# Hybrid S5 / gMLP trunk: second-token transposes inside a product, last columns in two parts, S5 tiles pipelined, x on the ScalarE queue, first products by quarters

## The chip, the cores and the metric

One Trainium2 chip, one of its cores. The metric is device time in microseconds (us) of one execution. The kernel before took 971.5 us in the median of three runs (970.46 to 971.52).

## What is computed

The input x is 256 tokens by 1024 columns, float32. Two layers follow, each of three sub-layers of the form "residual plus branch, then layer normalisation" (cut from the reference):

```python
for i in range(DEPTH):                                    # DEPTH = 2
    h = _layernorm(DN_ALPHA * h + 0.5 * _swiglu(h, ffn_w_in[i, 0], ffn_w_out[i, 0]), ln_g[i, 0], ln_b[i, 0])
    mix = _s5_mixer(h, ...) if i % 2 == 0 else _gmlp_mixer(h, ...)
    h = _layernorm(DN_ALPHA * h + mix, ln_g[i, 1], ln_b[i, 1])
    h = _layernorm(DN_ALPHA * h + 0.5 * _swiglu(h, ffn_w_in[i, 1], ffn_w_out[i, 1]), ln_g[i, 2], ln_b[i, 2])

def _swiglu(x, w_in, w_out):                              # 1024 -> 2 x 2816 -> 1024
    gate, up = jnp.split(x @ w_in, 2, axis=-1)
    return (jax.nn.silu(gate) * up) @ w_out
```

The S5 mixer projects in, runs a diagonal complex state-space scan over the tokens, gates the result (`z = y * sigmoid(y @ w_glu + b_glu)`) and projects out. The gMLP mixer projects to u and v, normalises v, mixes its tokens with one 128x128 matrix per head, multiplies by u and projects out. So the order of sub-layers is FFN, S5, FFN, FFN, gMLP, FFN, and the six are called FFN0, S5, FFN1, FFN2, gMLP, FFN3 here.

## The kernel before, in words

**Numbers.** Every float32 product is made of three matmuls on operands split into a high part (rounded to the matmul's type) and a low part (the rest): high x high, high x low, low x high (`mm3`, L201 to L203, with 512 moving columns; `mm3t`, L208 to L210, with 256). The split of a weight block takes a cast on ScalarE (`hi`) and a subtraction on VectorE (`lo`).

**Tokens.** The 256 tokens are two tiles of 128 rows, t = 0 and t = 1, kept in `h[0]` and `h[1]`. A product needs the transposed tokens: `make_xt(t)` lets TensorE transpose eight 128x128 pieces into two PSUM tiles `tps` (L187), ScalarE casts each to the high part (L192), VectorE makes the low part (L193).

**Weights.** `Stream` keeps one list of weight blocks of 128x2048 for the whole program. SyncE's queue loads them (L63) into three `raw` buffers, `split` makes `hi` and `lo` (L88/L89 where the low part is put off to the next tick, `ws.lazy`; L96/L97 otherwise; L106/L107 in quarters at the start; L115/L119 slowly in S5). At most five split blocks are held. `ws.tick(n)` splits n more blocks if that bound allows and runs one piece of background work, which in FFN0 is the preparation of the S5 tables (VectorE L639 to L649, ScalarE L881 and others) and later that of the gMLP. Each engine works through its own queue strictly in the order in which the program was written (`manual_schedule`), so the place of a tick in the code decides what stands behind what.

**An FFN** goes through 11 chunks of 256 hidden units. Chunks 0 and 1 are computed token tile by token tile: in FFN0 by `start_in` (chunk 0) and `chunk_in(1)`, in the other FFNs by `step_in(0, 0)`, `step_in(1, 0)`, then `make_xt(1)`, then `step_in(0, 1)`, `step_in(1, 1)`, each of 8 input pieces k and hence 24 matmuls `ips`. In the second token tile `finish_g` transposes the gated values (L348) after the fourth k. From chunk 2 on weights are stationary (`chunk_in`, L208 to L210), and `step_out(c - 2)` adds a finished chunk to the accumulators `acc`. The last three chunks of the output product are done in `close`: first token tile 0, both halves of 512 columns, then token tile 1. The layer normalisation of a tile (VectorE L239, L240, L247, then L228, L231; GpSimd makes 1/sqrt in two steps, L221 and L222) starts when its halves are done. While TensorE is in token tile 1's last blocks, `make_xt(0)` already turns the normalised token tile 0 for the next sub-layer.

**The start of FFN0** (`start_in`): x and the first weight block come in pieces on SyncE's queue; `ws.early()` issues four small transposes `aps` for the S5 tables (L679, L680), whose results ScalarE copies out (L685 to L691).

**gMLP** begins with `step_v(0, 0)`, `step_v(1, 0)`, `make_xt(1)`, `act_v` of both, then `step_v` of token tile 1; its products are called `zps`.

**The end of S5**: after the gate products (`gacc`, L1148 to L1150) ScalarE makes eight tanh tiles (L1158), and `finish(n)` for n = 0 to 7 multiplies (L1164), casts to the high part (VectorE L1168 for n < 3, ScalarE L1170 from then on) and subtracts (L1171); `rest(1)` after n = 1 and 3 makes a half of a weight block's low part (L119). `close_mixer` then multiplies with `w_out`, in the order of k = n.

Of the kernel before, what the change touches and what calls it, by code (L numbers as in the profile page):

```python
# [16 lines left out]
P = 128  # L17
# [137 lines left out]
def hybrid(ctx: ExitStack, tc: tile.TileContext, a: dict, out: bass.AP, subs=SUBS):  # L155
# [63 lines left out]
    def rstd_of(mv, eps):  # L219
        rstd = st_p.tile([P, 2], F32, tag="rstd", name="rstd")  # L220
        nc.gpsimd.tensor_scalar(rstd[:, 0:1], mv[:, 1:2], eps, 1.0, op0=ALU.add, op1=ALU.mult)  # L221
        nc.gpsimd.tensor_tensor(rstd[:, 1:2], rstd[:, 0:1], mhalf, op=ALU.pow)  # L222
        return rstd[:, 1:2]
# [51 lines left out]

    def close(li, si, acc, blocks, mm, gb, hscale, eps, last):

        order = [(n, j) for n in range(2) for j in range(len(blocks))]
        for t in range(2):
            for n, j in order:  # L280
                for kt in range(2):
                    mm(j, t, n, kt, acc[t][n])
                    if (t, n, j, kt) == (1, 1, len(blocks) - 2, 0) and not last:
# [7 lines left out]
            if t == 1 and not last:  # L291
                ws.tick(1)
            layernorm(t, acc[t], gb, hscale, eps, sums)
            if t == 1 and not last and next_kind[li, si] != "s5":
                ws.tick(1, 4)
            if last:
                for n in range(2):
                    s = slice(512 * n, 512 * n + 512)
                    (nc.sync, nc.scalar)[n].dma_start(out=out[0, P * t:P * t + P, s], in_=h[t][:, s])

    def plan_ffn(li, fi, fine):
# [3 lines left out]
        def add_in(c):  # L305

            ids["in"][c] = []
            for kh in range(2):
# [11 lines left out]
                if step == 1 and kh == 0:  # L320
                    parts[2:2] = [(lambda raw: h[1], a["x"][0, P:2 * P, :])]
# [11 lines left out]
    def ffn(ids, li, si, first, last):  # L333
# [27 lines left out]
        def step_in(c, t):  # L361
            ps = mm_p.tile([P, 512], F32, tag="mm", name="ips")
            in_mm(ids["in"][c], t, ps, range(4))
            if t:
                finish_g()
            ws.tick()
            in_mm(ids["in"][c], t, ps, range(4, KD))
# [3 lines left out]
            ws.tick()  # L371

        def chunk_in(c):

            for m in range(2):
                ps = mm_p.tile([P, 2, SEQ], F32, tag="mm", name="ips")
                for g in range(2):
# [13 lines left out]
                    ws.tick()  # L391
# [17 lines left out]
        def start_in():  # L409
# [5 lines left out]
            split(0)  # L415
            make_xt(0, parts=[1])
            mm(0, 0)
            split(1)
            make_xt(1)
            ws.early()  # L420
            mm(0, 1)
            for k in range(2):
                mm(1, k)
            for k in range(2, 4):
                split(k)
                for t in range(2):
                    mm(t, k)
# [13 lines left out]
        def mm_out(c, t, n, kt, ps):  # L441
            gh, gl = (gts[c, kt][:, j, P * t:P * t + P] for j in range(2))
            wh, wl = ws.get(ids["out"][c])
            s = slice(D * kt + 512 * n, D * kt + 512 * n + 512)
            mm3(ps, gh, gl, wh[:, s], wl[:, s], c == 0 and kt == 0, c == NCH - 1 and kt == 1)
# [12 lines left out]
        if first:  # L458
            start_in()
            ws.lazy = True  # L460
            chunk_in(1)
        else:
            step_in(0, 0)
            step_in(1, 0)
            make_xt(1)
# [888 lines left out]
```

## Time and profile before

| | |
|---|---|
| median of three runs | 971.5 us |
| the profiled execution's own time | 971.83 us |
| its span in the profile | 969.7 us |
| TensorE busy in the span | 944.7 us (97%) |
| VectorE, ScalarE, GpSimd busy | 650.9, 426.5, 162.8 us |
| chain that ended last: TensorE, VectorE, ScalarE | 68%, 8%, 2% of the span |
| weight and other reads from HBM | 184.07 MB |

A row of the timeline gives start and duration in us, engine, line of the kernel, operation, output <- input, shape and count; behind it in brackets the idle time of that engine just before the row and what ended it. Matmuls overlap, so the distance from one start to the next says what a matmul costs, not its duration. PE is TensorE, DVE is VectorE, ACT is ScalarE, POOL is GpSimd, SP is SyncE.

### The profile page before, as it was taken

Reading aid. Unit: us, or ns where it says so; the run is one execution under the profiler, and the core shown is the slowest. Engines: PE = TensorE matmul, PEld = TensorE weight load, DVE = VectorE, ACT = ScalarE, POOL = GpSimd, SP = SyncE. Lnnn points to the kernel's source line nnn. Section 1 sums busy time; section 2 is a strip of 40 time slices with the busy share of each in tenths; the row PEclk is TensorE's granted clock in tenths of the full one; section 3 lists DMA queues with packets and bytes.
Section 4 is the critical chain, followed back from the end, with each engine's and each line's share of the span. In section 5 each row is a group of like instructions: output and inputs, shape, how many; then the busy total and the mean of one; then the engine's idle time right before and its main releaser. Section 6 shows DMA issues by size and latency. Waiting matters only on the chain.

```text
span 969.7 us, 16611 instructions
## 1 busy us (share of the span) xinstructions
PE 944.7 (97%) x6988; PEld 857.9 (88%) x6988; DVE 650.9 (67%) x805; ACT 426.5 (44%) x504; POOL 162.8 (17%) x240
## 2 busy tenths in 40 slices
PE   7999999999999999999999999999999999999996
PEld 5999999978896799999987999999889879999995
DVE  5889998787998774554667636455788866453635
ACT  5465347535342553434433534353445444444430
POOL 1888910011750100000001000000011010000001
PEclk9999999999999999999999999999999999999999
DMA  8887796958646566365547765636357468465521
GB/s 276 219 249 228 237 318 203 315 200 300 208 141 220 174 198 236 132 224 167 185 163 239 255 222 166 225 133 227 121 173 261 130 203 268 138 220 172 184 78 43
DMA packets 133898, 195.10 MB, mean 201 GB/s; under 512 B 7632, under 2 KB 104576, under 8 KB 133824
## 3 DMA queue, kind: packets, MB, share of 16 engines
q1 hardware_dynamic: 129152, 182.61, 56.8%
q0 software_dynamic: 4384, 10.92, 3.9%
q8 instruction: 54, 0.88, 0.4%
q10 hardware_dynamic: 288, 0.52, 0.1%
q14 instruction: 20, 0.16, 0.0%
HBM read 184.07 MB, written 9.96 MB: 200 GB/s over the span
## 4 chain that ended last, share of the span: by engine, by line
PE 68%; DVE 8%; ACT 2%; issue 1%; POOL 1%; DMA 1%; POOLq 0%; DVEq 0%; ACTq 0%
PE ips L210 11%; PE ips L209 11%; PE ips L208 11%; PE acc L201 7%; PE acc L202 7%; PE acc L203 7%; DVE lo L97 3%; PE pps L1080 2%; PE ips L203 1%; ACT hi L96 1%; DVE lo L89 1%; DMA raw<-in_s_w_in 1%; PE ips L201 1%; PE ips L202 1%; PE zps L209 1%
## 5 line engine op out<-in xcount | busy, mean ns | idle before, releaser
L210 PE MATMUL ips<-xt,lo 128*128 128x256 f32 x1184 | 335.2, 283 | 2.2 <-DVE lo L89 2.2
L208 PE MATMUL ips<-xt,hi 128*128 128x256 f32 x1184 | 335.4, 283 | 0.0
L209 PE MATMUL ips<-xt,hi 128*128 128x256 f32 x1184 | 335.0, 283 | 0.0
L89 DVE TENSOR_TENSOR lo<-raw,hi 128x2048 fp32r<-128x2048 f32 x107 | 242.9, 2291 | 8.7 <-ACT hi L88 8.3
L210 PEld LDWEIGHTS ips<-xt,lo 128*128 128x128 f32 x1184 | 227.1, 192 | 2.6 <-DVE lo L89 2.6
L208 PEld LDWEIGHTS ips<-xt,hi 128*128 128x128 f32 x1184 | 227.1, 192 | 1.5
L209 PEld LDWEIGHTS ips<-xt,hi 128*128 128x128 f32 x1184 | 227.1, 192 | 1.4
L88 ACT CAST hi<-raw 128x2048 fp32r<-128x2048 f32 x107 | 203.9, 1909 | 46.4 <-PE acc L203 26.6
L398 DVE TENSOR_TENSOR sgg<-ips,sgg 128x256 f32<-128x256 f32 x74 | 31.1, 420 | 166.1 <-ACT sgg L397 166.0
L201 PE MATMUL acc<-hi,gt 128*128 128x512 f32 x352 | 137.9, 392 | 0.2 <-ACT gt L406 0.2
L202 PE MATMUL acc<-lo,gt 128*128 128x512 f32 x352 | 137.4, 390 | 0.0
L203 PE MATMUL acc<-hi,gt 128*128 128x512 f32 x352 | 137.0, 389 | 0.0
L397 ACT ACTIVATE sgg<-ips 128x256 f32<-128x256 f32 x74 | 28.4, 383 | 216.4 <-PE ips L210 213.5
L221 POOL TENSOR_SCALAR rstd<-mv 128x1 f32<-128x1 f32 x14 | 10.4, 741 | 634.6 <-DVE mv L247 610.8
L97 DVE TENSOR_TENSOR lo<-raw,hi 128x2048 fp32r<-128x2048 f32 (+2 forms) x52 | 89.6, 1754 | 22.7 <-ACT hi L96 22.6
L203 PEld LDWEIGHTS acc<-hi,gt 128*128 128x128 f32 x352 | 66.1, 188 | 14.3 <-DVE gt L407 0.2
L201 PEld LDWEIGHTS acc<-hi,gt 128*128 128x128 f32 x352 | 66.2, 188 | 13.2 <-ACT gt L406 0.6
L202 PEld LDWEIGHTS acc<-lo,gt 128*128 128x128 f32 x352 | 66.3, 188 | 12.2
L96 ACT CAST hi<-raw 128x2048 fp32r<-128x2048 f32 (+2 forms) x52 | 74.5, 1482 | 4.2 <-DMA raw<-in_ffn_w_in 2.5
L407 DVE TENSOR_TENSOR gt<-sgg,gt 128x256 fp32r<-128x256 f32 x74 | 32.4, 438 | 61.8 <-ACT gt L406 61.8
L406 ACT CAST gt<-sgg 128x256 fp32r<-128x256 f32 x74 | 30.1, 406 | 58.2 <-DVE sgg L398 58.2
L201 PE MATMUL ips<-hi,xt 128*128 128x512 f32 x112 | 46.0, 410 | 3.6 <-ACT xt L192 2.3
(229 smaller groups left out, 1222.1 us busy)
## 6 DMA issues: line engine op xcount, KB each, us to landing
raw<-in_ffn_w_in SPq DMA_DIRECT2D x172, 512.0 KB, 5.7
raw<-in_ffn_w_out SPq DMA_DIRECT2D x44, 1024.0 KB, 5.1
raw<-in_g_w_in SPq DMA_DIRECT2D x8, 1024.0 KB, 6.0
rows<-w SPq DMA_DIRECT2D x8, 512.0 KB, 6.3
raw<-in_s_w_in SPq DMA_DIRECT2D x4, 1024.0 KB, 8.4
raw<-in_s_w_glu SPq DMA_DIRECT2D x4, 1024.0 KB, 5.0
w<-rows SPq DMA_DIRECT2D x8, 512.0 KB, 5.8
tc<-tc SPq DMA_DIRECT2D x16, 256.0 KB, 5.5
```

The source lines that it names most:

```text
L88: nc.scalar.copy(hi, raw)
L89: self.unfinished.append(lambda: nc.vector.tensor_tensor(lo, raw, hi.bitcast(F32), op=ALU.subtract))
L96: nc.scalar.copy(hi[:, s], raw[:, s])
L97: eng[p % len(eng)].tensor_tensor(lo[:, s], raw[:, s], hi[:, s].bitcast(F32), op=ALU.subtract)
L201: nc.tensor.matmul(ps, xh, wh, start=start, stop=False)
L202: nc.tensor.matmul(ps, xh, wl, start=False, stop=False)
L203: nc.tensor.matmul(ps, xl, wh, start=False, stop=stop)
L208: nc.tensor.matmul(ps, wh, xh, start=start, stop=False)
L209: nc.tensor.matmul(ps, wh, xl, start=False, stop=False)
L210: nc.tensor.matmul(ps, wl, xh, start=False, stop=stop)
L398: nc.vector.tensor_tensor(g, ps[:, 1], sg, op=ALU.mult)
L407: nc.vector.tensor_tensor(x[:, 1], g, x[:, 0].bitcast(F32), op=ALU.subtract)
```

## The change

Five groups of edits.

1. *Start.* x is loaded by three DMAs on ScalarE's queue, no longer on SyncE's among the weight pieces. `start_in` multiplies each quarter of the first weight block with token tile 0 as soon as it is split, turns token tile 1 only after that, and issues `ws.early()` after token tile 1's four products. `ws.lazy` is set one step later, inside `chunk_in(1)`, and that step splits two blocks at once.
2. *Second tokens.* In `step_in(1, 0)` and `step_v(1, 0)` the call `make_xt(1)` stands after the fifth of the eight k. Before it no new block is split (`split=0` in `step_in(0, 0)` and `step_v(0, 0)`).
3. *1/sqrt.* The first of the two steps (add eps) is done by VectorE instead of GpSimd, in all 14 normalisations.
4. *End of S5.* The subtraction of tile n is issued after the multiplication of tile n + 1; for n = 3 and 5 GpSimd does it; the products z lie in four buffers instead of two; the halves of the weight split come after n = 4 and 5.
5. *Last sub-layer.* `close_last` makes columns 512 to 1023 of token tile 1 in two products of 256 columns, which go to PSUM tiles of their own (`ops`) for the last three chunks; what the accumulator held before is added to the residual ahead of them. Statistics, normalisation and output of that tile are in parts too.

```diff
 def rstd_of(mv, eps):
-    nc.gpsimd.tensor_scalar(rstd[:, 0:1], mv[:, 1:2], eps, 1.0, op0=ALU.add, op1=ALU.mult)
+    nc.vector.tensor_scalar(rstd[:, 0:1], mv[:, 1:2], eps, 1.0, op0=ALU.add, op1=ALU.mult)
     nc.gpsimd.tensor_tensor(rstd[:, 1:2], rstd[:, 0:1], mhalf, op=ALU.pow)
...
+def close_last(acc, blocks, mm, gb, hscale, eps):
+    for t in range(2):
+        parts = [(0, 512), (512, 512)] if t == 0 else [(0, 512), (512, 256), (768, 256)]
+        step = parts[-1][1]
+        if t == 1:
+            s = slice(512, D)
+            nc.vector.scalar_tensor_tensor(r[:, s], in0=h[t][:, s], scalar=hscale, in1=acc[t][1], op0=ALU.mult, op1=ALU.add)
+        for i, (c, w) in enumerate(parts):
+            ps = acc[t][n] if w == 512 else mm_p.tile([P, 512], F32, tag="mm", name="ops")[:, 0:w]
+            for j in range(len(blocks)):
+                for kt in range(2):
+                    mm(j, t, n, kt, ps, (c % 512, w), w < 512 and j == 0 and kt == 0)
...
-def step_in(c, t):
+def step_in(c, t, mid=None, split=1):
     ps = mm_p.tile([P, 512], F32, tag="mm", name="ips")
-    in_mm(ids["in"][c], t, ps, range(4))
+    cut = 5 if mid else 4
+    in_mm(ids["in"][c], t, ps, range(cut))
+    if mid:
+        mid()
     if t:
         finish_g()
-    ws.tick()
-    in_mm(ids["in"][c], t, ps, range(4, KD))
+    ws.tick(split)
+    in_mm(ids["in"][c], t, ps, range(cut, KD))
     in_act(c, t, ps)
     if t == 1:
         done(ids["in"][c])
-    ws.tick()
+    ws.tick(split)
...
-                    ws.tick()
+                    if first and (c, m, g) == (1, 0, 0):
+                        ws.tick(2)
+                        ws.lazy = True
+                    else:
+                        ws.tick()
...
             split(0)
+            mm(0, 0)
             make_xt(0, parts=[1])
-            mm(0, 0)
-            split(1)
+            for k in range(1, 4):
+                split(k)
+                mm(0, k)
             make_xt(1)
+            for k in range(4):
+                mm(1, k)
             ws.early()
-            mm(0, 1)
-            for k in range(2):
-                mm(1, k)
-            for k in range(2, 4):
-                split(k)
-                for t in range(2):
-                    mm(t, k)
...
-            step_in(0, 0)
-            step_in(1, 0)
-            make_xt(1)
+            step_in(0, 0, split=0)
+            step_in(1, 0, lambda: make_xt(1))
...
-        pend = [step_v(0, 0), step_v(1, 0)]
-        make_xt(1)
+        pend = [step_v(0, 0, split=0), step_v(1, 0, lambda: make_xt(1))]
...
-            z = buf["o"][n % 2][:, 0].rearrange("p q k -> p (q k)")
+            z = buf["o"][n % 2][:, n // 2 % 2].rearrange("p q k -> p (q k)")
...
-            V.tensor_tensor(yx(n, 1), z, yx(n, 0).bitcast(F32), op=SUB)
+            return lambda: (G if n in (3, 5) else V).tensor_tensor(yx(n, 1), z, yx(n, 0).bitcast(F32), op=SUB)
...
+        second = lambda: None
         for n in range(CT):
-            finish(n)
-            if n in (1, 3):
+            x = finish(n)
+            second()
+            second = x
+            if n in (4, 5):
                 rest(1)
+        second()
...
-            nc.sync.dma_start(out=h[0][:, s], in_=a["x"][0, 0:P, s])
-        if kinds[0] != "ffn":
-            nc.sync.dma_start(out=h[1], in_=a["x"][0, P:2 * P, :])
+            nc.scalar.dma_start(out=h[0][:, s], in_=a["x"][0, 0:P, s])
+        nc.scalar.dma_start(out=h[1], in_=a["x"][0, P:2 * P, :])
```

How the instructions stand afterwards is shown at three places. The first is ScalarE's queue at the very start: `xt` are the tokens' casts, `hi_154` the four quarters of weight block 0, `hi_222` those of block 1, and the rows on `aps` the copies for the S5 tables. Before:

```order
L192 CAST xt<-tps 128x512
L106 CAST hi_154<-raw_101 128x512
L192 CAST xt<-tps 128x512
L106 CAST hi_154<-raw_101 128x512
L192 CAST xt<-tps 128x512 x2
L676 COPY s5a<-dt_131 32x128
L685 COPY ch<-aps 128x64
L687 COPY ldt<-aps 128x32
L690 COPY dg<-aps 128x8
L691 ACTIVATE dg<-aps 128x8
L106 CAST hi_154<-raw_101 128x512 x2
```

and with the change, where the token tile 1 casts, and with them the copies, come after all four quarters:

```order
L192 CAST xt<-tps 128x512
L106 CAST hi_154<-raw_102 128x512
L192 CAST xt<-tps 128x512
L106 CAST hi_154<-raw_102 128x512 x3
L192 CAST xt<-tps 128x512 x2
L713 COPY s5a<-dt_131 32x128
L722 COPY ch<-aps 128x64
L724 COPY ldt<-aps 128x32
L727 COPY dg<-aps 128x8
L728 ACTIVATE dg<-aps 128x8
L106 CAST hi_222<-raw_107 128x512 x4
```

The copies and the quarters of block 1 behind them now wait for the casts of token tile 1 and for `aps`, where before only two quarters of block 0 stood between.

The second place is TensorE at the same start. `h_95` is token tile 1, and `aps` the transposes whose results ScalarE copies. Before, from the third matmul of the first product on:

```order
L203 MATMUL ips<-hi_154,xt 128x512
L187 MATMUL tps<-ident,h_95 128x128 x8
L679 MATMUL aps<-ident,s5a 128x32 x3
L680 MATMUL aps<-ident,s5a 128x16
L201 MATMUL ips<-hi_154,xt 128x512
L202 MATMUL ips<-lo_155,xt 128x512
L203 MATMUL ips<-hi_154,xt 128x512
```

and with the change, from the last product of token tile 1 with block 0 on:

```order
L201 MATMUL ips<-hi_154,xt 128x512
L202 MATMUL ips<-lo_155,xt 128x512
L203 MATMUL ips<-hi_154,xt 128x512
L716 MATMUL aps<-ident,s5a 128x32 x3
L717 MATMUL aps<-ident,s5a 128x16
L201 MATMUL ips<-hi_222,xt 128x512
L202 MATMUL ips<-lo_223,xt 128x512
L203 MATMUL ips<-hi_222,xt 128x512
```

What moved is `aps`: nine matmuls of token tile 0 and twelve of token tile 1 with block 0 are now ahead of it, and the first matmul with block 1 stands right behind it.

The third place is VectorE at the entry of FFN1. The four 128x512 rows are the quarters of the second block of chunk 1, the 128x2048 row is the next whole block. Before:

```order
L231 SCALAR_TENSOR_TENSOR h_95<-r,rstd,bet 128x512 x2
L97 TENSOR_TENSOR lo_3723<-raw_3589,hi_3722 128x512 x4
L97 TENSOR_TENSOR lo_3751<-raw_3602,hi_3750 128x2048
L358 TENSOR_TENSOR sgg<-ips,sgg 128x256 x2
L193 TENSOR_TENSOR xt<-tps,xt 128x512 x2
L352 TENSOR_TENSOR gt<-tps,gt 128x128 x4
```

and with the change, where that whole block stands behind the two `xt` rows, and the second gated product `sgg` behind the block:

```order
L231 SCALAR_TENSOR_TENSOR h_95<-r,rstd,bet 128x512 x2
L97 TENSOR_TENSOR lo_3723<-raw_3589,hi_3722 128x512 x4
L390 TENSOR_TENSOR sgg<-ips,sgg 128x256
L193 TENSOR_TENSOR xt<-tps,xt 128x512 x2
L97 TENSOR_TENSOR lo_3796<-raw_3602,hi_3795 128x2048
L390 TENSOR_TENSOR sgg<-ips,sgg 128x256
L384 TENSOR_TENSOR gt<-tps,gt 128x128 x4
```

The whole block went from ahead of both gated products and the token rows to between the token rows and the second gated product.

More of the change, by code (lines that the diff above doesn't have):

```diff
@@ L276, in close @@
     def close(li, si, acc, blocks, mm, gb, hscale, eps, last):
+        if last:
+            return close_last(acc, blocks, mm, gb, hscale, eps)
         order = [(n, j) for n in range(2) for j in range(len(blocks))]
@@ L282, in close @@
                     mm(j, t, n, kt, acc[t][n])
-                    if (t, n, j, kt) == (1, 1, len(blocks) - 2, 0) and not last:
+                    if (t, n, j, kt) == (1, 1, len(blocks) - 2, 0):
                         make_xt(0, next_kind[li, si] == "s5")
@@ L290, in close @@
                     sums = layernorm_half(t, acc[t][0], 0, hscale)
-            if t == 1 and not last:
+            if t == 1:
                 ws.tick(1)
             layernorm(t, acc[t], gb, hscale, eps, sums)
-            if t == 1 and not last and next_kind[li, si] != "s5":
+            if t == 1 and next_kind[li, si] != "s5":
                 ws.tick(1, 4)
[L296 to L299, printed above, removed]
     def plan_ffn(li, fi, fine):
@@ L439, in start_in, with mm_out @@
             done(ids["in"][0])
-        def mm_out(c, t, n, kt, ps):
+        def mm_out(c, t, n, kt, ps, cols=(0, 512), start=False):
             gh, gl = (gts[c, kt][:, j, P * t:P * t + P] for j in range(2))
             wh, wl = ws.get(ids["out"][c])
-            s = slice(D * kt + 512 * n, D * kt + 512 * n + 512)
-            mm3(ps, gh, gl, wh[:, s], wl[:, s], c == 0 and kt == 0, c == NCH - 1 and kt == 1)
+            s = slice(D * kt + 512 * n + cols[0], D * kt + 512 * n + sum(cols))
+            end = NCH - 4 if last and (t, n) == (1, 1) and cols[1] == 512 else NCH - 1
+            mm3(ps, gh, gl, wh[:, s], wl[:, s], start or c == 0 and kt == 0, c == end and kt == 1)
         def step_out(c, t):
@@ L479, in ffn @@
         c0 = NCH - 3
-        close(li, si, acc, [ids["out"][c] for c in range(c0, NCH)], lambda j, t, n, kt, ps: mm_out(c0 + j, t, n, kt, ps),
+        close(li, si, acc, [ids["out"][c] for c in range(c0, NCH)], lambda j, *args: mm_out(c0 + j, *args),
               gb, 2 * ALPHA, 4 * EPS, last)
```

37 lines of the change are left out of this document (29 added, 8 removed).

## Prediction

> **What bounds the kernel now.** I read the page's busy times first, then a table of windows, then the timeline where a window loses TensorE time. The page says:
>
> ```profile
> span 969.7 us, 16611 instructions
> PE 944.7 (97%) x6988; PEld 857.9 (88%) x6988; DVE 650.9 (67%) x805; ACT 426.5 (44%) x504; POOL 162.8 (17%) x240
> ```
>
> TensorE is busy 944.7 of 969.7 us. The change removes no product, so only TensorE's 25 us of idle time, and matmuls that run slowly, are to be had. The windows (span, then busy PE, PEld, DVE, ACT, POOL) show where:
>
> ```profile
> 0.00:16.00 16.00, 10.35 (x32) 7.55 (x33) 6.81 (x11) 8.49 (x18) 3.61 (x13) 1.00 0.88 267
> 290.00:305.00 15.00, 13.39 (x60) 9.57 (x59) 10.88 (x22) 6.40 (x14) 0.00 (x0) 1.00 0.73 232
> 305.00:340.00 35.00, 33.27 (x154) 26.61 (x153) 27.13 (x37) 14.83 (x20) 4.46 (x6) 1.00 0.56 180
> 940.00:970.00 30.00, 21.29 (x114) 18.12 (x112) 12.92 (x22) 1.20 (x3) 3.38 (x4) 0.93 0.09 35
> ```
>
> The start idles 5.7 us, the end of S5 1.6, the entry of FFN1 1.7 and the end 8.7; the entries of S5, FFN2 and gMLP are single waits, quoted below. The change touches each. The sum is made against the profiled execution, 971.83 us (span 969.7 and 2.1 around it). The median is 0.33 lower; I lower the result by the same.
>
> **Second tokens.** At the entry of FFN2, TensorE turns token tile 1, then waits for its casts:
>
> ```profile
> 515.83 4.69 DVE L97 TENSOR_TENSOR lo<-raw,hi 128x512 fp32r<-128x512 f32 x5
> 520.44 0.75 DVE L358 TENSOR_TENSOR sgg<-ips,sgg 128x256 f32<-128x256 f32 x2
> 518.99 0.40 PE L203 MATMUL ips<-hi,xt 128*128 128x512 f32 x1
> 519.22 1.03 PE L187 MATMUL tps<-ident,h 128*128 128x128 f32 x8
> 519.86 1.07 ACT L192 CAST xt<-tps 128x512 fp32r<-128x512 f32 x2
> 521.01 0.47 PE L201 MATMUL ips<-hi,xt 128*128 128x512 f32 x1 [0.75 <-ACT xt L192]
> 521.84 0.50 PE L203 MATMUL ips<-hi,xt 128*128 128x512 f32 x1
> 711.96 0.50 PE L201 MATMUL zps<-hi,xt 128*128 128x512 f32 x1 [0.96 <-DVE xt L193]
> ```
>
> Matmuls of 512 columns stand 0.23 apart (518.99, 519.22). From 519.22 to 521.84 are 2.62 us for eight transposes (0.9) and two matmuls (0.46): 1.3 lost. Turned after the fifth k, the transposes start nine matmuls (2.05 us) earlier, at 517.1, and the casts are done at 517.1 + 0.64 + 1.07 = 518.8, while nine matmuls run to 520.1. VectorE has the four quarters (4.69 less one whole block of 2.29) by 518.2, one gated product by 518.5, both token rows by 519.9. So the second tile's product starts at 520.1 and waits for nothing: 1.4 us gained with the small gaps.
>
> But a new wait comes. The whole block (2.29) now stands between the token rows and the second gated product. ScalarE casts it at 518.8 to 520.7, VectorE splits it to 523.0, the product follows to 523.4. `finish_g` wants it after twelve matmuls, at 522.8: 0.5 lost. So 0.95 at each FFN entry behind another sub-layer, and three of them: **2.85**, between 0 (the block's load late) and 4.2 (no new wait). At gMLP nothing of the second product is wanted there: the 0.96 of idle goes, and an estimated 0.2 by which the first matmuls behind such a wait run slower (0.50 against 0.40), **1.15**, between 0.9 and 1.3.
>
> **1/sqrt.** GpSimd's first step goes to VectorE:
>
> ```profile
> 501.44 0.21 DVE L247 BATCH_NORM_AGGREGATE mv<-bst 128x2 f32<-128x12 f32 x1
> 501.69 1.42 DVE L228 SCALAR_TENSOR_TENSOR r<-r,mv,gam 128x512 f32<-128x512 f32 x2
> 503.56 1.42 DVE L231 SCALAR_TENSOR_TENSOR h<-r,rstd,bet 128x512 f32<-128x512 f32 x2 [0.46 <-POOL rstd L222]
> ```
>
> VectorE idles 0.46 before L231. The new row is 128x1; the nearest are L247 (0.21, next start 0.25 later) and the 128x32 rows below (0.17). At 0.22 it delays L228 by as much, GpSimd is then no longer the later one, and 0.24 is left. Bounds 0.1 and 0.35. It counts only where TensorE waits for a normalisation: the entry of S5, the entry of FFN1, the end.
>
> **End of S5.** The rows of `finish`, and what TensorE loses by them:
>
> ```profile
> 291.35 0.40 PE L201 MATMUL acc<-hi,xt 128*128 128x512 f32 x1
> 303.14 0.42 DVE L1171 TENSOR_TENSOR xt<-rot,xt 128x256 fp32r<-128x256 f32 x1 [0.53 <-ACT xt L1170]
> 303.16 0.50 PE L201 MATMUL acc<-hi,xt 128*128 128x512 f32 x1 [0.52 <-ACT xt L1170]
> 304.95 2.29 DVE L97 TENSOR_TENSOR lo<-raw,hi 128x2048 fp32r<-128x2048 f32 x1 [1.39 <-ACT hi L96]
> 313.97 0.39 PE L203 MATMUL acc<-hi,xt 128*128 128x512 f32 x1
> 315.14 1.29 PE L187 MATMUL tps<-ident,h 128*128 128x128 f32 x8 [0.78 <-DVE h L231]
> 283.72 1.43 POOL L1132 TENSOR_TENSOR xt<-y,xt 128x256 fp32r<-128x256 f32 x1 [3.81 <-ACT xt L1125]
> ```
>
> VectorE waits 0.53 for ScalarE's cast in each of tiles 3 to 7, and all eight subtractions (0.42) stand on it, to 303.56. Pipelined, four of the five waits are covered by the next multiplication and two subtractions are GpSimd's: 2.1 + 0.8 = 2.9 sooner, 300.6. TensorE has 42 matmuls from 291.35 up to the last one with tile 7, at 0.23 each 9.6, but needs until 303.96. Subtractions 0 and 1 come one multiplication later than now, which I put at 1.1 of waiting, so it is done at 302.0: 2.0 gained. GpSimd's rows (1.43 by the row shown) are wanted more than 2 us after they end. The blocks at 304.95 and the normalisation behind them come 2.9 sooner, 0.24 more by 1/sqrt, so token tile 0 can be turned at 312.0 instead of 315.14; TensorE, whose last matmul before that ends at 314.2, gets there at 312.2. So the wait of 0.94 goes too: **3.0** in all. Bounds 2.0 (that wait stays) and 3.2.
>
> **End.** Columns in two parts of 256:
>
> ```profile
> 961.33 0.69 DVE L239 SCALAR_TENSOR_TENSOR r<-h,acc 128x512 f32<-128x512 f32 x1 [1.85 <-PE acc L203]
> 962.05 0.69 DVE L240 BATCH_NORM_STATS2 bst<-r 128x6 f32<-128x512 f32 x1
> 964.89 1.41 DVE L231 SCALAR_TENSOR_TENSOR h<-r,rstd,bet 128x512 f32<-128x512 f32 x2 [0.44 <-POOL rstd L222]
> ```
>
> Of 256 columns, L239 and L240 should take 0.42 each (an estimate; below 0.69, above L247's 0.21): 0.55 less, and 1/sqrt 0.24. Against it 36 matmuls at 0.12 (24.64 to 24.87 below, the third of a group) replace 18 at 0.23: 0.2 more. The last store is half as large, 0.0 to 0.2. Sum **0.6**, bounds 0.1 and 1.1.
>
> **Start and FFN0.** Here I expect a loss:
>
> ```profile
> 4.61 0.58 ACT L192 CAST xt<-tps 128x512 fp32r<-128x512 f32 x1 [2.60 <-PE tps L187]
> 6.06 0.62 ACT L106 CAST hi<-raw 128x512 fp32r<-128x512 f32 x1 [0.87 <-DMA raw<-in_ffn_w_in]
> 12.16 0.80 PE L201 MATMUL ips<-hi,xt 128*128 128x512 f32 x1
> 16.60 0.49 PE L202 MATMUL ips<-lo,xt 128*128 128x512 f32 x1
> 24.64 0.28 PE L208 MATMUL ips<-xt,hi 128*128 128x256 f32 x1
> 24.87 0.28 PE L210 MATMUL ips<-xt,lo 128*128 128x256 f32 x1
> 13.25 3.70 DVE L107 TENSOR_TENSOR lo<-raw,hi 128x512 fp32r<-128x512 f32 x6 [0.93 <-ACT hi L106]
> 16.87 0.17 DVE L645 TENSOR_SCALAR ex<-ldt 128x32 f32<-128x32 f32 x1
> 19.42 2.29 DVE L97 TENSOR_TENSOR lo<-raw,hi 128x2048 fp32r<-128x2048 f32 x1
> 26.28 0.17 DVE L645 TENSOR_SCALAR n<-ch 128x32 f32<-128x32 f32 x1
> 39.89 0.39 PE L210 MATMUL ips<-xt,lo 128*128 128x256 f32 x1 [1.46 <-DVE lo L89]
> 206.72 1.01 PE L187 MATMUL tps<-ident,h 128*128 128x128 f32 x6 [1.53 <-DVE h L231]
> ```
>
> Today TensorE runs without a break from 12.16 to 24.64: 45 matmuls, 0.43 apart until 16.60, 0.23 from then on. With the change the first load may land 0.9 earlier, but ScalarE casts the tokens until 5.2 anyway, so quarter 0 is ready at 5.8 and the first product ends near 7.5. The second half of token tile 0 is turned behind it and cast by 9.2, the other quarters by 11, and their nine matmuls at the slow pace end at 14.1. Token tile 1 is turned and cast by 15.8, its twelve matmuls end at 18.9, `aps` at 19.3. Only then ScalarE makes the copies and casts block 1 (20.3), and VectorE its low part (21.0). The 23 matmuls left end at 26.2: 1.5 late. VectorE's last quarter is done at 22.9 where it was 16.95; the S5 steps (16.87 to 19.42) come next, so the low parts that chunk 1 wants at once are ready at 27.6 and 29.9: 1.2 and 0.8 of waiting. Then the 1.6 lost at 39.89 goes, since those two blocks now stand ahead of the S5 steps of 26.28. Their second has its raw buffer only at 27.6; with a load of some 6 us, a cast and the S5 steps the gated product of chunk 1 comes at about 41, and chunk 2 at 39.8 waits for its PSUM: 0 to 2, I take 1. At 42 us TensorE is 2.9 late. What follows has idle time that can take some of it back, most at 206.72, where TensorE waits 1.53 for a normalisation that hangs on VectorE and the loads. I carry **+1.2** into S5, less than half, with the 0.24 in it. Bounds: -0.2 (all taken back) and +3.6 (nothing).
>
> The clock of the start: the pitch halves at 16.60, 4.4 us after the unbroken run began. The Trainium skill, page "TensorE: Matmul & The Clock Gate", section "What's actually happening", gives a free-running window of about 3.4 us of sustained work instead. By it the run from 10.65 would be fast at 14.1 rather than 15.1, and the first term an estimated 0.4 smaller; one execution cannot show the window's phase.
>
> The Trainium skill, page "DMA: Bandwidth & Descriptors", section "Issuing engines are not separate DMA queues", speaks against the x queue: issuing from two engines saves only sequencer time. The trace of before, with its first loads all on SyncE, cannot show it, and the sum takes nothing from that queue.
>
> **Sum.** +1.2 - 3.0 - 2.85 - 1.15 - 0.6 = -6.4: 971.83 becomes 965.4, and 0.33 lower **965.1** as a median.
>
> **Rivals.** *S5's tables become the bound (slower).* The S5 steps of 26.28 start behind two more blocks, near 37: 10.5 late. If they set the entry of S5, with no slack, the sum is 971.5 + 10.5 - 7.6 = 974.4. It decides where the entry comes over 9.5 us late (7.6 and 1.9), that is with less than 1 us of slack. Against it: GpSimd saw the last table stored at 188.35, 18 us ahead of 206.72.
>
> ```profile
> 188.35 0.53 POOL L216 DMA_DIRECT2D bet<-in_ln_b  x1 [7.79 <-DMA kd<-k]
> ```
>
> *The new wait eats the turn.* If the whole block's load or cast comes 1 us later, the three FFN entries gain nothing: 968.0. For it: those entries wait for ScalarE and VectorE today, and both queues stay in order. *The start's loss stays whole*: +3.6 instead of +1.2, 967.5; for it, VectorE stands behind both waits of chunk 1 and behind the 1.46 at 39.89. *The loss is taken back whole*: 963.7; for it, the 1.53 at 206.72.
>
> **Chances.** Forecast 0.50, wait eats the turn 0.17, loss whole 0.12, loss taken back 0.15, tables 0.06. A measurement of this kernel tells 0.2% (1.9 us) from no change. Only the tables' case is slower; mixtures of the two middle ones reach no change: faster 0.88, same 0.05, slower 0.07. The range 962.0 to 969.0 takes in all but the tables' case and the far ends.
>
> **What would show it.** Right: no idle time before the second tile's first product, but 0.3 to 0.7 before L348's second half; TensorE done with S5's 42 matmuls 2 us sooner and no wait for token tile 0 after it; a hole of over 1 us at the first matmul of block 1, right behind `aps`. Wrong: S5 entered later than 209 or sooner than 206.5; FFN entries with more than 1 us of idle.

## The result and the profile after

The changed kernel took 965.7 us in the median of six runs (964.31 to 966.62), the kernel before 972.41 in six: the three named above and three more, of 973.3 to 975.4. The ratio is 0.9928, 95% interval 0.991 to 0.9946: 5.3 to 8.8 us less. The forecast was 6.4 us less, 965.1. The profiled execution took 965.24, its span is 963.4 instead of 969.7. One execution of the first variant further down took 3276 us; its ratio leaves that one out. The page's head and busy times:

```profile
span 963.4 us, 16652 instructions
...
PE 942.2 (98%) x7006; PEld 858.7 (89%) x7006; DVE 650.9 (68%) x822; ACT 425.6 (44%) x504; POOL 151.3 (16%) x228
```

TensorE's idle time fell from 25 to 21.2 us. The windows of before, again (span, then busy PE, PEld, DVE, ACT, POOL; the last one is shorter because the program ends there):

```profile
0.00:16.00 16.00, 9.70 (x30) 6.46 (x30) 4.21 (x7) 5.67 (x10) 3.59 (x13) 1.00 0.93 303
290.00:305.00 15.00, 14.57 (x79) 12.10 (x79) 12.95 (x22) 9.30 (x17) 5.10 (x5) 1.00 0.63 199
305.00:340.00 35.00, 34.81 (x165) 28.76 (x164) 28.63 (x40) 14.49 (x21) 3.08 (x4) 1.00 0.65 215
940.00:963.40 23.40, 15.86 (x87) 13.65 (x86) 13.15 (x27) 0.41 (x1) 1.85 (x2) 0.92 0.13 46
```

The end of S5 and the entry of FFN1 idle 0.4 and 0.2 us now (1.6 and 1.7 before). The start idles 6.3 instead of 5.7. To see what each place is worth I match the same matmuls in both traces and take the difference of their starts; what it changes by between two places is what that stretch gained or lost:

| stretch, up to | before | after | difference | stretch | forecast |
|---|---|---|---|---|---|
| entry of S5, first `tps` | 206.72 | 208.96 | +2.24 | +2.24 | +1.2 |
| S5 itself, first `acc` with `w_out` | 291.35 | 293.90 | +2.55 | +0.31 | 0 |
| end of S5, FFN1's first `ips` | 318.34 | 317.59 | -0.75 | -3.30 | -3.0 |
| turn in FFN1 | 340.46 | 338.57 | -1.89 | -1.14 | -0.95 |
| turn in FFN2 | 538.93 | 535.82 | -3.11 | -1.22 | -0.95 |
| turn in gMLP | 744.88 | 740.37 | -4.51 | -1.40 | -1.15 |
| turn in FFN3 | 831.39 | 825.73 | -5.66 | -1.15 | -0.95 |
| end of the span | 969.7 | 963.4 | -6.3 | -0.64 | -0.6 |

So the sum, -6.3, came out as forecast (-6.4), with a start that lost 1.0 more than thought, 0.3 lost inside S5, and an end of S5 and turns that gained 1.2 more. The start in the timeline:

```profile
14.96 1.07 ACT L192 CAST xt<-tps 128x512 fp32r<-128x512 f32 x2 [3.77 <-PE tps L187]
...
19.27 0.21 ACT L722 COPY ch<-aps 128x64 f32<-128x64 f32 x1 [3.06 <-PE aps L717]
...
19.58 2.20 ACT L106 CAST hi<-raw 128x512 fp32r<-128x512 f32 x4
20.27 0.50 PE L201 MATMUL ips<-hi,xt 128*128 128x512 f32 x1 [1.04 <-ACT hi L106]
...
26.35 0.28 PE L208 MATMUL ips<-xt,hi 128*128 128x256 f32 x1
...
27.56 0.39 PE L210 MATMUL ips<-xt,lo 128*128 128x256 f32 x1 [0.82 <-DVE lo L97]
...
29.76 0.39 PE L210 MATMUL ips<-xt,lo 128*128 128x256 f32 x1 [0.51 <-DVE lo L97]
...
162.76 0.39 PE L210 MATMUL ips<-xt,lo 128*128 128x256 f32 x1 [1.09 <-DVE lo L89]
```

ScalarE idles 3.06 us until `aps` is through, and only then casts block 1; TensorE waits 1.04 for that behind `aps`. Blocks 0 and 1 are done at 26.35 (24.64 before), and the two waits of chunk 1 for its low parts follow. The wait of 1.46 at 39.89 is gone. A wait for VectorE at 162.76 has grown from 0.74 to 1.09.

The entry of FFN2, where before TensorE stood 0.75 between the turn and the second product:

```profile
515.08 1.03 PE L187 MATMUL tps<-ident,h 128*128 128x128 f32 x8
515.87 0.47 PE L201 MATMUL ips<-hi,xt 128*128 128x512 f32 x1
...
518.64 2.29 DVE L97 TENSOR_TENSOR lo<-raw,hi 128x2048 fp32r<-128x2048 f32 x1 [1.02 <-ACT hi L96]
520.85 0.42 DVE L390 TENSOR_TENSOR sgg<-ips,sgg 128x256 f32<-128x256 f32 x1
...
520.75 0.38 PE L380 MATMUL tps<-ident,sgg 128*128 128x128 f32 x2
521.32 0.44 PE L380 MATMUL tps<-ident,sgg 128*128 128x128 f32 x2 [0.20 <-DVE sgg L390]
```

The turn goes over into the product without a break. The new wait is there, 0.20 of idle, for the gated product that stands behind the whole block on VectorE.

### The profile page after: what moved, and what is told of

It is laid out like the page before. It is cut to its first block, busy times and chain, and to the rows that moved or that the text cites. A ratio compares the mean times of both kernels' runs of the same rounds, so it can differ in the third digit from the quotient of the medians.

```text
span 963.4 us, 16652 instructions
## 1 busy us (share of the span) xinstructions
PE 942.2 (98%) x7006; PEld 858.7 (89%) x7006; DVE 650.9 (68%) x822; ACT 425.6 (44%) x504; POOL 151.3 (16%) x228
## 4 chain that ended last, share of the span: by engine, by line
PE 75%; DVE 2%; ACT 1%; POOL 0%; issue 0%; DVEq 0%; POOLq 0%; ACTq 0%
PE ips L210 11%; PE ips L209 11%; PE ips L208 11%; PE acc L203 8%; PE acc L201 8%; PE acc L202 8%; PE ips L203 2%; PE ips L201 2%; PE ips L202 2%; PE pps L1117 2%; PE tps L187 1%; PE zps L210 1%; PE zps L209 1%; PE zps L208 1%; PE ups L203 1%; PE ups L201 1%
## 5 line engine op out<-in xcount | busy, mean ns | idle before, releaser
L89 DVE TENSOR_TENSOR lo<-raw,hi 128x2048 fp32r<-128x2048 f32 x105 | 238.5, 2294 | 7.2 <-ACT hi L88 7.0
L88 ACT CAST hi<-raw 128x2048 fp32r<-128x2048 f32 x105 | 200.4, 1910 | 37.5 <-PE acc L203 26.6
L202 PE MATMUL acc<-lo,gt 128*128 128x512 f32 x346 | 135.2, 391 | 0.2 <-DVE lo L89 0.2
L201 PE MATMUL acc<-hi,gt 128*128 128x512 f32 x346 | 135.4, 391 | 0.0
L203 PE MATMUL acc<-hi,gt 128*128 128x512 f32 x346 | 134.7, 389 | 0.0
L97 DVE TENSOR_TENSOR lo<-raw,hi 128x2048 fp32r<-128x2048 f32 (+2 forms) x54 | 94.3, 1775 | 27.9 <-ACT hi L96 27.8
L222 POOL TENSOR_TENSOR rstd<-rstd,mhalf 128x1 f32<-128x1 f32 x14 | 13.3, 950 | 625.6 <-DVE rstd L221 625.6
L96 ACT CAST hi<-raw 128x2048 fp32r<-128x2048 f32 (+2 forms) x54 | 78.7, 1501 | 6.3 <-DMA raw<-in_ffn_w_in 4.3
L203 PEld LDWEIGHTS acc<-hi,gt 128*128 128x128 f32 x346 | 65.0, 188 | 13.8
L201 PEld LDWEIGHTS acc<-hi,gt 128*128 128x128 f32 x346 | 65.1, 188 | 12.4
```

What stands on the lines that cost most here:

```text
L88: nc.scalar.copy(hi, raw)
L89: self.unfinished.append(lambda: nc.vector.tensor_tensor(lo, raw, hi.bitcast(F32), op=ALU.subtract))
L96: nc.scalar.copy(hi[:, s], raw[:, s])
L97: eng[p % len(eng)].tensor_tensor(lo[:, s], raw[:, s], hi[:, s].bitcast(F32), op=ALU.subtract)
L201: nc.tensor.matmul(ps, xh, wh, start=start, stop=False)
L202: nc.tensor.matmul(ps, xh, wl, start=False, stop=False)
```

## The experiments

Ratios are to the kernel before, runs beside runs, with 95% intervals; "with the change" means 0.9928. Since the differences between variants are about as large as the spread of single executions, the trace decides, by the same matmuls. Behind the start they repeat well: the entry of FFN2 takes 26.73 to 26.76 us in all seven traces that share it. The start itself scatters. The four traces with the start as changed lie within 1.5 us of each other at 172 us (0.42 sooner to 1.04 later than the profiled one), and the four with the old start within 0.5 (2.55 to 3.02 sooner). So a smaller difference of two starts isn't shown by one trace of each.

### What the start costs, and why

First the whole of group 1 undone, groups 2 to 5 kept:

```diff
-            mm(0, 0)
             make_xt(0, parts=[1])
-            for k in range(1, 4):
-                split(k)
-                mm(0, k)
+            mm(0, 0)
+            split(1)
             make_xt(1)
...
-            nc.scalar.dma_start(out=h[0][:, s], in_=a["x"][0, 0:P, s])
+            nc.sync.dma_start(out=h[0][:, s], in_=a["x"][0, 0:P, s])
```

> The changed kernel with its whole first group undone (x on SyncE's queue, the old order of the first products, low parts put off from chunk 1 on); groups 2 to 5 stay. Theory: the new start costs TensorE 2.15 us at 45 us and 3.0 at 175 us (acc and kps rows of the two traces), and since the 1.5 us wait at the entry of S5 hangs on TensorE's own last product, it passes that loss on unchanged. So token tile 0 is turned for S5 at 206.4 to 206.7 instead of 208.96, everything behind moves by 2.2 to 2.5, and the time is about 963.2. Rival: waits further on (S5's entry, 245 us) pay the start's loss back anyway; then S5 is entered 2 us sooner but the end moves by less than 1 us, 964.7 or more.

Measured: 962.5 us, 0.9900 (0.9883 to 0.9918). TensorE is 1.33 sooner at 52 us, 2.55 at 176 us, 3.42 at the entry of S5, and the span ends 2.8 sooner. The last step, from 2.55 to 3.42, is chance: the weight block on which that entry hangs (see below) landed 0.86 sooner here, counted from the same matmul. Another 0.7 is lost again at 285 us, where TensorE waits 0.45 for a row of GpSimd; four of the 14 traces have that wait. The start as changed is a loss, and it is not paid back further on: the rival falls.

Next, the suspected cause alone, the place of `aps`:

```diff
-            for k in range(4):
+            mm(1, 0)
+            ws.early()
+            for k in range(1, 4):
                 mm(1, k)
-            ws.early()
```

> The changed kernel with the four small transposes aps issued behind the first of token tile 1's four products with block 0 instead of behind the fourth. Theory: the copies of aps, and the casts of block 1 queued behind them on ScalarE, are what delays block 1; they come 2.0 us sooner, the 1.04 wait at 20.27 goes, the low parts of chunk 1 come 2 us sooner too and its two waits (0.82 and 0.51) stay near 0.4 and 0.6; TensorE is 1.8 to 2.1 us sooner at 34 us and the time falls by 1.5 to 2.5, to about 963.6. Rival: block 1 is late because it lands or is split late whatever stands before it; then less than 0.5 us is gained at 34 us.

Measured: 962.83 us, 0.9908 (0.9889 to 0.9926). The first matmul with block 1 needs no wait, TensorE is 1.58 sooner at 34 us, 1.91 at 52 us and 3.25 at 172 us; the span ends 2.4 sooner.

```profile
17.66 0.21 ACT L723 COPY ch<-aps 128x64 f32<-128x64 f32 x1 [1.00 <-PE aps L718]
...
17.98 2.20 ACT L106 CAST hi<-raw 128x512 fp32r<-128x512 f32 x4
...
19.73 0.39 PE L201 MATMUL ips<-hi,xt 128*128 128x512 f32 x1
```

The casts of block 1 begin at 17.98 instead of 19.58, and its first matmul, at 19.73, follows without idle time. Moving four small transposes takes back nearly all that the whole start had lost.

Then the old order with x on SyncE's queue, but low parts put off one step later, as in the change:

> The changed kernel with x back on SyncE's queue and the first products in the old order, but chunk 1's low parts still made at once, two blocks in one step, and put off only from the next step on. Theory: the old order enters chunk 1 at 24.7 instead of 26.35, and the 1.6 us wait at 39.89 of the kernel before does not come back, so TensorE is up to 3 us sooner at 45 us than with the change and S5 is entered near 205 to 206; time 961.5 to 963. Rival: with low parts at once, the S5 steps that stand ahead of them on VectorE delay chunk 1 by the same 1.5 us that are saved at 39.89; then it equals the variant with the whole old start, 963.2.

Measured: 961.15 us, 0.9887 (0.9868 to 0.9905). TensorE does not wait once between 26 and 60 us, is 2.34 sooner than with the change at 52 us and 4.10 at 172 us; the span ends 4.0 sooner. Of group 1, this edit is worth having: against the whole old start it is 1.0 sooner at 52 us, though token tile 1 landed 1.2 later in this execution, because the old start's wait (1.46 of idle at 40.70) is not there. The rival falls by the trace; the medians, 1.35 apart with intervals that overlap, don't show it.

Last, x alone back on SyncE's queue:

> The changed kernel with x back on SyncE's queue between the weight pieces; all else as changed. Theory: the weight pieces behind x land 0.8 us later, so the first product starts near 6.7 instead of 5.94, the quarters behind it are late by 0.8 to 1.2 and block 1, which waits for token tile 1's products, too; time 0.5 to 1.0 longer, 966.5. Rival: the queue matters only for its issue time and the first products wait for the transposes and casts; then the first product moves and nothing behind 27 us does, 965.7.

Measured: 965.8 us, 0.9933 (0.9916 to 0.9949); unclear. In the profiled execution the first product starts at 7.57 instead of 5.94 and TensorE is 1.69 late at 52 us, but the median stands 0.1 from that of the change (this execution is the slowest of its six), and a part of the loss belongs to the clock:

```profile
20.00:23.00 3.00, 1.73 (x9) 0.97 (x8) 1.07 (x2) 2.05 (x8) 0.00 (x0) 0.98 0.00 1
23.00:26.00 3.00, 3.00 (x8) 2.34 (x8) 2.76 (x11) 3.00 (x3) 0.00 (x0) 0.50 0.09 12
```

After the wait behind `aps` the granted clock (the third figure from the end) fell to 0.50; in the same windows of the changed kernel, behind a wait of the same 1.04, it stayed 1.00:

```profile
20.00:23.00 3.00, 2.50 (x10) 1.85 (x11) 2.71 (x6) 3.00 (x5) 0.00 (x0) 1.00 0.00 0
23.00:26.00 3.00, 3.00 (x15) 2.49 (x14) 2.66 (x12) 2.98 (x3) 0.00 (x0) 1.00 0.60 176
```

The queue does not decide this. The variant tested next, at the entry of S5, has the start of the change, and there the clock fell as well behind a wait of 1.04:

```profile
23.00:26.00 3.00, 3.00 (x9) 2.37 (x8) 2.62 (x14) 2.98 (x3) 0.00 (x0) 0.56 0.43 119
```

That trace reaches chunk 1 at 28.54, 2.19 later than the changed kernel's, but is only 0.40 late at 45 us: chunk 1 then finds its low parts ready, and its two waits are gone. So what x on ScalarE's queue is worth at the end stays open. At the start it shows: the first product begins at 5.7 to 6.2 us in the six traces with x there, and at 6.7 to 7.6 in the eight with x on SyncE's queue.

### The entry of S5

Of the loss at 172 us, 3.02, the entry of S5 kept 2.24, although TensorE waits there 1.29 us. The timeline of the changed kernel shows what for:

```profile
199.52 1.91 ACT L96 CAST hi<-raw 128x2048 fp32r<-128x2048 f32 x1 [2.03 <-DMA raw<-in_s_w_in]
...
201.46 2.29 DVE L97 TENSOR_TENSOR lo<-raw,hi 128x2048 fp32r<-128x2048 f32 x1 [1.65 <-ACT hi L96]
203.67 0.68 DVE L239 SCALAR_TENSOR_TENSOR r<-h,acc 128x512 f32<-128x512 f32 x1
...
206.67 0.15 DVE L221 TENSOR_SCALAR rstd<-mv 128x1 f32<-128x1 f32 x1
206.75 1.40 DVE L228 SCALAR_TENSOR_TENSOR r<-r,mv,gam 128x512 f32<-128x512 f32 x2
208.07 1.41 DVE L231 SCALAR_TENSOR_TENSOR h<-r,rstd,bet 128x512 f32<-128x512 f32 x2
...
208.96 1.23 PE L187 MATMUL tps<-ident,h 128*128 128x128 f32 x8 [1.29 <-DVE h L231]
```

A weight block lands, ScalarE casts it, VectorE splits it, and the normalisation stands behind that on VectorE. From the cast to the turn are 9.44 us. It is 9.43 to 9.45 in all nine traces with 1/sqrt on VectorE and this order, and 9.93 or 9.94 in the three with 1/sqrt on GpSimd (196.78 to 206.72 before), whether TensorE waits 0.42 or 3.05. The landing comes 31.6 to 33.8 us after the first of the `kps` matmuls of FFN0, which starts between 158.5 and 168.7 in these traces. SyncE issues the load 22.2 to 22.4 us after that matmul in all 14 traces, when VectorE's L89 has freed the buffer, and it lands 8.8 to 11.3 us later. So the issue is tied to TensorE's own progress, TensorE's lateness comes back as a late landing, and the time of the load adds over two microseconds of chance. The 0.78 that the change did get back here are the 0.50 of 1/sqrt and 0.28 of this chance (landed 32.50 after that matmul, 32.78 before). The experiment splits that block behind the normalisation:

```diff
                 if t == 0 and n == 0 and j < 2:
-                    ws.tick()
+                    ws.tick(next_kind[li, si] != "s5")
...
             layernorm(t, acc[t], gb, hscale, eps, sums)
+            if t == 0 and next_kind[li, si] == "s5":
+                ws.tick()
```

> The changed kernel with one difference at the entry of S5: the weight block that is split on VectorE ahead of token tile 0's normalisation is split behind it. Theory: TensorE waits there (1.29 with the change, 1.53 before) because that block has just landed and its 2.29 us on VectorE stand ahead of the normalisation; in seven traces token tile 0 is turned 9.44 us (9.94 with 1/sqrt on GpSimd) after ScalarE begins that block's cast, whatever TensorE does. With the block behind it the wait goes whole, TensorE passes from its last product to the turn in 0.3, and the time is 1.2 to 1.5 less, 964.3; the loss of the start is then passed on by TensorE itself. Rival: the normalisation is late because of its own length (4.9 us from the last product of token tile 0); then at most 0.3 goes. A second: the block comes 7 us later and the first products of S5 wait for it, which gives the 1.3 back.

Measured: 963.08 us, 0.9910 (0.9895 to 0.9926); the span is 2.2 shorter. The timeline:

```profile
206.85 0.39 PE L203 MATMUL acc<-hi,gt 128*128 128x512 f32 x1
207.09 0.60 PE L187 MATMUL tps<-ident,h 128*128 128x128 f32 x4
...
204.25 1.41 DVE L231 SCALAR_TENSOR_TENSOR h<-r,rstd,bet 128x512 f32<-128x512 f32 x2
205.57 2.29 DVE L97 TENSOR_TENSOR lo<-raw,hi 128x2048 fp32r<-128x2048 f32 x1
```

TensorE goes from its last product to the turn in 0.24. Of the 1.87 gained at that place, 0.42 was there before (at 173 us), and 1.45 is the wait with the delay around it. S5's first products do not wait for the block. Both rivals fall.

### The turns and the end of S5

The wait that the change brought at the FFN entries, taken away by splitting the next block later:

```diff
-            ws.tick(split)
+            ws.tick(0 if mid else split)
             in_mm(ids["in"][c], t, ps, range(cut, KD))
...
-            ws.tick(split)
+            ws.tick(2 if mid else split)
```

> The changed kernel with one difference at the entries of FFN1, FFN2 and FFN3: the next whole weight block is split behind the second gated product instead of ahead of it. Theory: the wait that the change brought (0.20 of idle at L380 and slower matmuls around it, 0.36 in all) exists because the block's 2.29 us stand ahead of the second gated product on VectorE; it goes at all three entries, and the block still comes over 4 us before chunk 2 wants it: 0.9 to 1.1 less, 964.6. Rival: the block, 2 us later, makes chunk 2 wait, or takes up ScalarE when the gated values are to be cast; then nothing is gained or 1 to 2 us are lost.

Measured: 964.33 us, 0.9925 (0.9911 to 0.9938). In the profiled execution the start happened to be 0.95 later; from there the three entries gain 0.41, 0.40 and 0.43, to 0.33 sooner at the end. At FFN2 the four transposes now go as one:

```profile
521.04 0.39 PE L203 MATMUL ips<-hi,xt 128*128 128x512 f32 x1
521.27 0.60 PE L380 MATMUL tps<-ident,sgg 128*128 128x128 f32 x4
521.63 0.48 PE L201 MATMUL ips<-hi,xt 128*128 128x512 f32 x1
```

Nothing in chunk 2 waits for the later block. By the medians alone, 1.4 us apart, this could not be told.

The second group alone, on the kernel before (its `step_in` and `step_v` as in the change):

> The kernel before with the second group alone (token tile 1 turned inside the second product of FFN1, FFN2, FFN3 and of gMLP). Theory: this group's gain is its own, by the trace of the whole change 1.15, 1.22, 1.15 and 1.40: 4.9 less than the kernel before, 966.6 to 967.1; by the prediction 4.0, 967.8. Rival: at the entries the quarters of VectorE that follow the normalisation are on time only because 1/sqrt and the end of S5 are faster too; then it gains under 3.5.

Measured: 967.1 us, 0.9958 (0.9943 to 0.9972), 2.7 to 5.5 less than before. In the trace the turns of FFN1, FFN2, gMLP and FFN3 gain 1.05, 1.10, 1.18 and 1.02, together 4.35: most of the 4.9 is this group's own; the other half microsecond it had only together with the other groups. The profiled execution itself lost 1.6 at the entry of S5, where that block landed 33.75 after `kps` and TensorE waited 3.05.

The fourth group alone, on the kernel before:

> The kernel before with the fourth group alone (end of S5). Theory: by the trace of the whole change 3.3 are gained up to FFN1's first product, of which the wait of 0.94 for the normalisation of token tile 0 goes only as far as the chain to it gets shorter by more than TensorE does: TensorE's 42 products end 2.4 sooner, the chain 3.0 sooner, so 0.3 of that wait is left without the 0.5 of 1/sqrt; 2.8 to 3.1 less than the kernel before, 968.6. Rival: the wait for the normalisation takes back what TensorE gains and only 2.0 or less is left.

Measured: 968.55 us, 0.9971 (0.9958 to 0.9983). In the trace the stretch from the first product with `w_out` to FFN1's first gains 2.98, and nothing of the wait for the normalisation of token tile 0 is left, also without the faster 1/sqrt. By the trace the rival of 2.0 falls; the interval of the medians, 1.6 to 4.1 less than before, would still allow it.

Within this group GpSimd's part was in doubt. The changed kernel around its two rows:

```profile
298.16 1.14 DVE L1201 SCALAR_TENSOR_TENSOR rot<-rot,y 128x256 f32<-128x256 f32 x1
...
300.61 1.61 DVE L1201 SCALAR_TENSOR_TENSOR rot<-rot,y 128x256 f32<-128x256 f32 x2
302.29 0.83 DVE L1208 TENSOR_TENSOR xt<-rot,xt 128x256 fp32r<-128x256 f32 x2
...
296.98 1.85 POOL L1208 TENSOR_TENSOR xt<-rot,xt 128x256 fp32r<-128x256 f32 x1 [6.05 <-issue]
299.87 1.41 POOL L1208 TENSOR_TENSOR xt<-rot,xt 128x256 fp32r<-128x256 f32 x1 [1.04 <-ACT xt L1207]
```

```diff
-            return lambda: (G if n in (3, 5) else V).tensor_tensor(yx(n, 1), z, yx(n, 0).bitcast(F32), op=SUB)
+            return lambda: V.tensor_tensor(yx(n, 1), z, yx(n, 0).bitcast(F32), op=SUB)
```

> The changed kernel with all eight subtractions of the end of S5 on VectorE, none on GpSimd. Theory: GpSimd's two rows (1.85 and 1.41) slow VectorE's multiplications beside them (1.14 for one and 1.61 for two, where one alone takes 0.62), so that giving them to GpSimd gained nothing; without it the last subtraction ends within 0.2 of where it does now, 9.1 us after the first product with w_out, and the time stays. Rival: the two rows of 0.42 come back on VectorE, its chain is 0.8 longer, and token tile 0's normalisation and turn are 0.5 to 0.8 later.

Measured: 964.77 us, 0.9931 (0.9919 to 0.9943). From the entry of S5 to the end of the program every matched matmul stands within 0.04 us of the changed kernel. VectorE's multiplications are short again, and its last subtraction ends 0.4 sooner than with GpSimd's help:

```profile
298.50 0.62 DVE L1201 SCALAR_TENSOR_TENSOR rot<-rot,y 128x256 f32<-128x256 f32 x1
298.95 0.42 DVE L1208 TENSOR_TENSOR xt<-rot,xt 128x256 fp32r<-128x256 f32 x1
...
302.32 0.43 DVE L1208 TENSOR_TENSOR xt<-rot,xt 128x256 fp32r<-128x256 f32 x1 [0.28 <-ACT xt L1207]
```

So the pipelining is what gains; GpSimd's two rows cost VectorE as much as they take from it. The Trainium skill, page "SBUF — State Buffer", section "Who interferes with whom", says that a VectorE instruction with two inputs in SBUF contends with a GpSimd instruction that reads SBUF, and that the order of issue decides who is blocked. The rows agree in part: L1201 and L1208 both have two such inputs, and L1201 at 298.16 takes 1.14 beside GpSimd's row where it takes 0.62 alone. Which of two is held back they don't settle: VectorE's L119 at 297.03, in the same stretch as GpSimd's first row, takes 1.22, as long as without that row (1.21).

### Put together

The combination: groups 2 to 5, the old order of the first products with low parts put off one step later, the next block behind the second gated product, no subtraction on GpSimd, x on SyncE's queue:

> Groups 2 to 5 of the change with the old order of the first products and x on SyncE's queue, low parts put off one step later, the next whole block behind the second gated product at the FFN entries, no subtraction on GpSimd. Theory: the gains add up: the variant with low parts put off one step later (961.15) less 1.24 for the three entries, 959.9. Rival: they share a cover further on, such as the load that sets the entry of S5, and less than 0.5 is left of the entries' gain, 960.7 or more.

Measured: 959.07 us, 0.9865 (0.9847 to 0.9883). Against the variant with low parts put off one step later the three entries gain 0.41, 0.40 and 0.46, so they share no cover and the rival falls. The rest of the 2.3 between the two spans is the start, where token tile 1 landed 1.5 sooner in this execution with the same instructions: chance.

The same with x on ScalarE's queue:

> The same combination with x on ScalarE's queue instead of SyncE's. Theory: with the weight pieces no longer behind x the quarters of block 0 come 0.8 to 1.1 sooner, and TensorE, which in this order waits for the quarters up to 12 us, is 0.5 to 1.2 sooner at 45 us; time up to 1 less than with x on SyncE's queue. Rival: in this order token tile 1 is wanted early, and it shares the engines of the loads with the weights in either case; then nothing moves by more than 0.3.

Measured: 958.15 us, 0.9857 (0.9838 to 0.9876). TensorE turns token tile 1 at 7.68 instead of 9.00 and is 2.9 sooner at 53 us in the trace, but this execution is the fastest of its four, and most of the 2.9 is TensorE's pace: its matmuls of 512 columns stand 0.23 apart from 11.08 on, in the other trace only from 16.16 on (0.43 until then). The medians differ by 0.9 and the intervals overlap, so a gain in time by the queue is not shown. In traces with the old order and x on SyncE's queue that turn begins between 9.00 and 10.54 and always waits for the landing of x; here it is the earliest of all.

And with the block at the entry of S5 moved as well (x on SyncE's queue):

> The combination with x on SyncE's queue and, in addition, the block at the entry of S5 split behind the normalisation. Theory: 1.0 to 1.3 less than the combination without it, 958.8, and less spread from execution to execution, since the landing of that block no longer sets the entry. Rival: the first products of S5 wait for the block instead; then no difference.

Measured: 957.13 us, 0.9840 (0.9820 to 0.9859). The 1.99 that TensorE waited at the entry of S5 in the combination are gone. The profiled execution, the slowest of the five, is no shorter for it (span 957.4, without the move 957.1): token tile 1 was turned 1.25 later, and a block of FFN0's output weights landed late. Its low part stands ahead of gated values on VectorE, for which TensorE lost 1.6 before the entry.

```profile
192.22 0.50 PE L201 MATMUL acc<-hi,gt 128*128 128x512 f32 x1 [0.81 <-ACT gt L449]
```

The medians say 1.9 less, and their intervals overlap. The spread did not get smaller as expected (954.45 to 959.2). This is the fastest median; the version with both this move and x on ScalarE's queue was not run.

## Why the prediction was right, step by step

**The start** was the step that failed in size: +1.2 carried into S5, measured +2.24. S5 was entered at 208.96, just short of the 209 that was to count as wrong. Its beginning held: chunk 1 was reached at 26.35 (forecast 26.2), its two waits took 0.98 and 0.66, with 0.2 more in the matmuls behind them (1.2 and 0.8), the 1.6 at 39.89 went. The wait of chunk 2 for its PSUM, put at 1, was 0.3, so TensorE was 2.15 late at 45 us, behind all this, not 2.9. What failed is the sentence after that, that the idle time further on takes more than half of it back, "most at 206.72, where TensorE waits 1.53 for a normalisation that hangs on VectorE and the loads". It does hang on the load, but the load follows TensorE; that wait moves along with the loss. And on the way VectorE, 3.0 late with its S5 steps, made TensorE wait 0.9 more at 154 and 163 us: a small piece of the rival in which the tables become the bound (its S5 steps came at 37.7, where near 37 was forecast, but VectorE had made up all but 3.0 by 126 us). At 172 us the loss was 3.02 of the 3.6 of the rival in which it stays whole.

**1/sqrt** was put at 0.24 and is worth 0.50 where TensorE waits for a normalisation (9.94 against 9.44). The new row takes 0.15 but delays the next by only 0.08, where I took 0.22, so the whole gap in front of L231 closes.

**Inside S5** nothing was forecast, and 0.31 is lost. All of it lies at 246 us, in the changed kernel and in every variant with the third group, and in none of the three traces without it; the cause stays open.

**Second tokens**: 1.4 gained by the turn, 0.5 lost to a new wait, was the forecast for each FFN entry. The new wait came at the row that was named, L380, for the reason that was named (removing it gave 0.41); it cost about 0.4 and not 0.5 (0.20 of it idle, where 0.3 to 0.7 was named). Each entry gained 1.14 to 1.22 instead of 0.95, and gMLP 1.40 instead of 1.15. The rival in which the new wait eats the turn falls.

**End of S5**: -3.30 against -3.0. TensorE waited twice for tiles 0 and 1, 0.20 and 0.23 of idle and 1.0 in all with the slower matmuls around and behind (forecast 1.1), then no more. It had its 42 matmuls 2.1 sooner (forecast 2.0), and up to FFN1's first product another 1.2, where the wait of 0.94 for token tile 0 had been counted. The credit given to GpSimd for two subtractions was wrong (nothing is gained by them), but VectorE's chain from the first product with `w_out` to its last subtraction shortened by 3.0 all the same (12.2 to 9.2), since the waits for ScalarE's cast were covered.

**End**: -0.64 against -0.6, but made up otherwise. The rows of 256 columns came out as estimated:

```profile
955.90 0.42 DVE L298 SCALAR_TENSOR_TENSOR r<-r,ops 128x256 f32<-128x256 f32 x1 [1.13 <-PE ops L203]
956.35 0.43 DVE L300 BATCH_NORM_STATS2 bst<-r 128x6 f32<-128x256 f32 x1
```

They save the 0.55 of the forecast. 1/sqrt saves nearly 0.5 here too, not 0.24, and the narrower products cost TensorE 0.33, not 0.2. So some 0.45 of the 0.64 is 1/sqrt, and about 0.2 is left for the columns in parts. This is read from the rows; neither group was run alone.

**In all** the mechanisms held at every place but one, the absorption behind the start. That the total came within 0.1 was luck: a loss 1.0 larger and 0.3 lost inside S5 met gains 1.2 larger.

## What to carry to other kernels

A wait in front of an engine is spare time for its own lateness only if what it waits for does not depend on that engine; a load whose buffer comes free by work that follows the late engine comes late with it. When small work is moved to a later place "because there is time", look at what is queued behind its consumers on the in-order engines: here four transposes of at most 32 columns held up a weight block on ScalarE for some 1.6 us. And split blocks behind, not ahead of, whatever the busy engine is waiting for: at both places where that was changed, the wait that the block had caused was gone.

## What the runs showed of the hardware

A wait of 1.04 us of TensorE was followed by about 3.4 us at half clock with x on SyncE's queue (matmuls 0.43 apart from 22.68 to 26.11, granted clock 0.50) and by no such stretch in the changed kernel's trace; a second trace with the changed kernel's start had one of 3.3 (22.47 to 25.78, granted clock 0.56). The Trainium skill, page "TensorE: Matmul & The Clock Gate", section "What's actually happening", explains such differences by a free-running window of about 3.4 us; the length of the slow stretches agrees, and so does it that the same instructions differ from one execution to the next. Why a wait as short as 1.04 us was enough the runs don't show. At the very beginning they differ as well: in the four traces with the changed start the matmuls speed up from 0.43 to 0.23 apart between 13 and 17 us (near 13 in the earliest, near 16.5 in the latest). The granted clock in the windows shows 1.00 all along there.

The landing of x at the start varied by 1.5 us from trace to trace, and the load of one weight block at the entry of S5, issued at the same point of the program, by 2.5 us from issue to landing. With the pace of the first matmuls these are three sources of the spread between executions of the same kernel, which at 2 to 5 us is larger than most of the edits compared here. How much of the spread each makes is not shown: with that load taken off the path of TensorE, it did not shrink.
